# A decoder block on one core: ten of 22 tiles of the down projection by seven-product blocks, and the low parts of six early up weights by an accumulating transfer

## The chip, the cores and the metric

The kernel runs on one core of a Trainium2 chip. The metric is the device time of the whole program in microseconds (us); the median of three runs is 874.54 us (873.18 to 876.31). The engines are PE (matmul; PEld is its weight load), DVE (elementwise, two inputs), ACT (elementwise, one input), POOL and SP; SP issues nearly all loads. SBUF is the on-chip memory, PSUM holds eight banks of matmul results.

## The reference, cut to what matters

A decoder block over 512 tokens of width 1024. Two parallel branches (a recurrence and an attention), merged, are followed by a feed-forward part with 2816 channels, and only that part is touched:

```python
h2 = rmsnorm(x, norm2_g[l]) * (1.0 + scale2) + shift2
u = causal_dwconv(h2 @ w_up[l], ffn_conv_w[l], ffn_conv_b[l])
u_gate, u_val = u[..., :D_FF], u[..., D_FF:]
x = x + gate2 * ((jax.nn.silu(u_gate) * u_val) @ w_down[l])
...
return rmsnorm(x, final_g)
```

All inputs and the output are float32.

## The kernel before

**Number format.** Each matmul operand is held as two tiles: a rounded high part and the rest, the low part. `split` makes them: ACT copies the source into the high part (L207), DVE subtracts the high part from the source (L208). A product then takes three matmuls: high x high, high x low, low x high (L239 to L241 in the projections, L837 to L839 and L1228 to L1230 in the down projection).

**Weights.** `Stream` loads raw weights of 128 x 1024 (512 KB) into one of three `raw` buffers and splits them into tiles of 512 columns, alternately under the tags `whl` and `whg`, with two buffers each. A tile is written when PE has finished with the tile that lay in its buffer before.

**The up projection.** The 2816 gate channels and 2816 value channels are computed in 22 steps j, each with one tile of 128 channels of either kind; the result of step j (`ff[j]`, 128 channels x 512 tokens, high and low) is the left side of the down projection. In seven steps (`STRASSEN`, j = 5, 7, ... 17) the two tiles are already computed together by seven products of quarter blocks with matmuls of 256 columns (L1099). The first four tiles are multiplied for 256 tokens at a time. DVE adds the convolution taps (L1151) and gates (L1155, L1156). From j = 18 on DVE also forms the gate row `g2` (L556).

**The down projection.** 512 tokens x 2816 channels times 2816 x 1024 weights. The output columns are done in two halves of 512. In the first half each of the 22 tiles of 128 channels is multiplied with four blocks of 128 tokens into four banks (12 matmuls of 512 columns a tile); then `resid2` multiplies by `g2` and adds to the residual `x1` (L1202, L1203), and the first half's part of the final norm follows (L1218 to L1220). In the second half the same is done into five pieces (`parts`: three token blocks, and the fourth in two halves of 256 columns). The last `LASTK` = 8 tiles are held whole (`wl`), so that each piece can be finished by itself: its evacuation and norm (L1250 to L1259) and its output transfer lie beside the next piece's matmuls.

**Order.** Up to the feed-forward part the order of every queue is a table of numbers (`QUEUES`), which the change leaves alone. In the feed-forward part the order comes from the framework's scheduler, which goes by priorities (`tc.high_priority(offset=...)`) and its own costs. So a change of the code there can move any instruction of the stage. Every engine runs its queue in order.

## Time and profile before

| | |
|---|---|
| median of three runs | 874.54 us |
| the profiled execution | 876.59 us |
| its span, first to last instruction | 874.8 us |
| mean granted PE clock | 0.993 |
| PE's matmul instructions | 4282 |
| up projection, first matmul of it | 500.45 us after the span's start |
| down projection, first matmul to last | 744.30 to 866.77 us |
| last output transfer issued behind | 869.51 us + 0.75 (last scaling on DVE) |

Each row of a timeline gives start, duration, engine, line of the code, operation, output <- inputs by the names of the program's tiles, and in brackets how long the engine had stood idle and what ended that. Lines are those of the kernel before. A row of a stretch gives its length, then the busy time of PE, PEld, DVE, ACT and POOL (with the number of instructions), the granted clock, the DMA engines' share and GB/s. Matmuls overlap each other in the pipeline, so their pace is read from start to start.

### The profile page before, as it was taken

The numbers are of one execution on the slowest core, as the hardware profiler recorded it, in microseconds if no ns is written. First come the engines' busy times: TensorE is split into PE (matmuls) and PEld (weight loads), VectorE is DVE, ScalarE is ACT, GpSimd is POOL, SyncE is SP. The second block draws the span as 40 slices with busy tenths as digits, with TensorE's granted clock in tenths as the row PEclk, the third lists the DMA queues.
The fourth block names the chain that finished last, engine by engine and source line by source line (L and its number), as shares of the span: only waits on it lengthen the run. The fifth ranks groups of instructions, "written<-read, shape, count | busy, mean of one in ns | idle before, by whom it ended". The sixth has DMA issues, their size and how long they took to land.

```text
span 874.8 us, 11864 instructions
## 1 busy us (share of the span) xinstructions
PE 852.0 (97%) x4282; PEld 695.0 (79%) x4282; DVE 682.4 (78%) x1298; ACT 513.5 (59%) x953; POOL 18.7 (2%) x43
## 2 busy tenths in 40 slices
PE   7999999999999999999999999999999999999996
PEld 3777888888876777777877897888888887888885
DVE  6988888998965999997465779999999899424434
ACT  7485878677755798885244565566666654322323
POOL 0001000000020000000000000000000000000000
PEclk8999999999999999999999999999999999999998
DMA  9913233344472333454324032122332374322212
GB/s 344 354 67 106 72 111 111 108 146 118 153 183 97 119 122 130 139 176 157 97 75 164 5 118 97 62 98 103 104 102 105 104 241 145 120 93 89 93 65 96
DMA packets 33805, 109.09 MB, mean 125 GB/s; under 512 B 4290, under 2 KB 8002, under 8 KB 33748
## 3 DMA queue, kind: packets, MB, share of 16 engines
q1 hardware_dynamic: 32116, 103.60, 34.9%
q0 software_dynamic: 1632, 4.75, 2.3%
q8 instruction: 33, 0.54, 0.2%
q14 instruction: 24, 0.20, 0.1%
HBM read 103.59 MB, written 2.13 MB: 121 GB/s over the span
## 4 chain that ended last, share of the span: by engine, by line
PE 52%; DVE 25%; ACT 9%; DMA 7%; issue 5%; POOL 0%; SPq 0%; ACTq 0%; DVEq 0%; POOLq 0%
DVE whg L208 4%; DVE whl L208 3%; DVE Y L1151 3%; PE tr L241 3%; PE tr L240 3%; PE tr L239 3%; PE acc L241 2%; PE acc L239 2%; PE acc L240 2%; DMA raw<-in_w_up 2%; PE acc L837 2%; PE acc L839 2%; PE acc L838 2%; PE tr L741 2%; PE tr L1228 2%
## 5 line engine op out<-in xcount | busy, mean ns | idle before, releaser
L208 DVE TENSOR_TENSOR whl<-raw,whl 128x512 fp32r<-128x512 f32 (+2 forms) x138 | 85.6, 624 | 49.7 <-ACT whl L207 49.3
L207 ACT ACTIVATE whl<-raw 128x512 fp32r<-128x512 f32 (+2 forms) x138 | 78.7, 577 | 77.2 <-PE tr L241 22.6
L208 DVE TENSOR_TENSOR whg<-raw,whg 128x512 fp32r<-128x512 f32 x126 | 85.7, 687 | 37.3 <-ACT whg L207 37.0
L207 ACT ACTIVATE whg<-raw 128x512 fp32r<-128x512 f32 x126 | 77.8, 625 | 57.1 <-PE fil L839 22.0
L718 ACT ACTIVATE P<-P,mx,qsc 128x512 f32<-128x512 f32 (+3 forms) x64 | 41.2, 645 | 17.4 <-DVE mx L714 17.4
L239 PE MATMUL acc<-A,whg 128*128 128x512 f32 x120 | 47.9, 399 | 0.0
L240 PE MATMUL acc<-A,whg 128*128 128x512 f32 x120 | 47.4, 395 | 0.0
L241 PE MATMUL acc<-A,whg 128*128 128x512 f32 x120 | 47.4, 395 | 0.0
L1151 DVE SCALAR_TENSOR_TENSOR Y<-acc,vec,Y 128x511 f32<-128x511 f32 (+1 forms) x58 | 42.9, 744 | 3.6 <-ACT Y L1149 3.5
L239 PE MATMUL acc<-A,whl 128*128 128x512 f32 x104 | 41.1, 396 | 0.1
L240 PE MATMUL acc<-A,whl 128*128 128x512 f32 x104 | 41.1, 395 | 0.0
L241 PE MATMUL acc<-A,whl 128*128 128x512 f32 x104 | 41.1, 395 | 0.0
L239 PE MATMUL gm<-A,whg 128*128 128x512 f32 x88 | 35.5, 404 | 0.0
L241 PE MATMUL gm<-A,whg 128*128 128x512 f32 x88 | 35.1, 399 | 0.2 <-DVE whg L208 0.2
L240 PE MATMUL gm<-A,whg 128*128 128x512 f32 x88 | 35.3, 401 | 0.0
L239 PE MATMUL tr<-A,whl 128*128 128x512 f32 x80 | 32.6, 408 | 1.4 <-ACT whl L207 1.4
L241 PE MATMUL tr<-A,whl 128*128 128x512 f32 x80 | 32.2, 402 | 1.6 <-DVE whl L208 1.4
L711 DVE CUSTOM_DVE_ANT_0 P<-acc,mask 128x384 f32<-128x384 f32 (+3 forms) x64 | 28.6, 485 | 4.5 <-PE acc L708 4.1
L240 PE MATMUL tr<-A,whl 128*128 128x512 f32 x80 | 31.6, 394 | 0.0
L208 DVE TENSOR_TENSOR pt<-tr,pt 128x512 fp32r<-128x512 f32 (+1 forms) x48 | 27.4, 596 | 2.2 <-ACT pt L207 1.6
L741 PE MATMUL tr<-pt,v 128*128 128x512 f32 (+3 forms) x128 | 28.2, 328 | 0.1
L207 ACT ACTIVATE ff<-Y 128x512 fp32r<-128x512 f32 x22 | 13.9, 631 | 23.8 <-DVE Y L1156 23.1
(555 smaller groups left out, 2482.3 us busy)
## 6 DMA issues: line engine op xcount, KB each, us to landing
raw<-in_w_up SPq DMA_DIRECT2D x44, 512.0 KB, 3.6
raw<-in_w_dn SPq DMA_DIRECT2D x22, 512.0 KB, 3.5
wa<-in_w_adat SPq DMA_DIRECT2D x16, 512.0 KB, 9.4
raw<-in_w_adat SPq DMA_DIRECT2D x16, 512.0 KB, 3.3
raw<-in_w_xr SPq DMA_DIRECT2D x10, 512.0 KB, 3.9
raw<-in_w_pr SPq DMA_DIRECT2D x10, 512.0 KB, 3.6
raw<-in_w_gm SPq DMA_DIRECT2D x8, 512.0 KB, 4.1
raw<-in_w_gr SPq DMA_DIRECT2D x8, 512.0 KB, 3.5
```

Source lines behind the costliest of these rows:

```text
L207: S.activation(h, src, AF.Copy)
L208: return V.tensor_tensor(dst[:, 1, lo_c:lo_c + n], src, h.bitcast(F32), SUB).ins
L239: PE.matmul(out, wh, x[:, 0, xs], start=start, stop=False)
L240: PE.matmul(out, wh, x[:, 1, xs], start=False, stop=False)
L241: return PE.matmul(out, wl, x[:, 0, xs], start=False, stop=stop).ins
L711: V.tensor_tensor_reduce(out=pt[:, POFF[qd]:POFF[qd] + n], in0=sc[qd], in1=mask[:, T - n:], scale=1.0, scalar=-3e38, op0=ADD, op1=ALU.max, ...
L718: S.activation(pq, pq, AF.Exp, scale=qsc[:, qb:qb + 1], bias=mx[:, qb:qb + 1], accum_out=sm[:, qb:qb + 1])
L741: PE.matmul(yb[:, kb * P:], vv, pth[:, part, off:off + n], start=(i == 0 and part == 0), stop=(i == 3 and part == 1))
L837: PE.matmul(out, lt[:, 0, s], w[:, 0, :], start=start, stop=False)
L838: PE.matmul(out, lt[:, 0, s], w[:, 1, :], start=False, stop=False)
L839: return PE.matmul(out, lt[:, 1, s], w[:, 0, :], start=False, stop=stop).ins
L1151: V.scalar_tensor_tensor(u[:, d:], src[:, :T - d], vc("fw", (2 - d) * 2 * NF + cj), u[:, d:], MUL, ADD)
```

## The change

It has three parts.

1. *Down projection.* Of the 22 tiles, the last ten (`DPAIRS` = 5 pairs, tiles 12 to 21) are taken out of both column halves' ordinary loops (`KO` = 12 tiles stay there). For each pair the left side is a block of 2 token halves x 2 tiles, the right side 2 tiles x 2 column quarters of 256, and the block product is done with seven products of 2 x 3 matmuls of 256 columns instead of eight. `f_forms` makes the sums of the left side once, on DVE and ACT, during the ordinary tiles of the first half; they replace half of the pair's first `ff` tile and fill `fs`, in the place of `h2` (tag `A`). `w_forms` makes the differences of the right side for each pair and column half, partly in place in the raw tile, and splits them. The seven products accumulate over the five pairs in seven banks; the combination (L1282 to L1290), gate and residual (L1294, L1296) follow once a round. The first half's round comes behind its ordinary tiles, the second half's round ahead of its ordinary tiles. The fourth sum's sign: the tile kept for product 4 is the negative of the usual form, so its product is added.
2. *Last tiles.* `LASTK` is 6 instead of 8; `wl` stands in the place of `fs`.
3. *Early up weights.* For six tiles (`ADDS`, the `whg` tiles 9, 11, ... 19 of the up weights, used in steps 2 to 4) the low part is not made by DVE: ACT copies the high part, copies it again with the sign changed into the low part's place, and POOL issues a transfer that adds the raw weights from DRAM to it.

```diff
-LASTK = 8
+LASTK = 6
+DPAIRS = 5
+ADDS = tuple(range(9, 20, 2))
+LATE = 100
...
-                split(w, 0, self.cut, self.raws[r][:, o:o + self.cut])
+                if u in self.adds:
+                    S.activation(w[:, 0, :self.cut], self.raws[r][:, o:o + self.cut], AF.Copy)
+                    S.activation(w[:, 1, :self.cut], w[:, 0, :self.cut].bitcast(F32), AF.Copy, scale=-1.0)
+                    G.dma_start(w[:, 1, :self.cut], self.dram[r][:, o:o + self.cut], accum_op=ADD)
+                else:
+                    split(w, 0, self.cut, self.raws[r][:, o:o + self.cut])
...
+        KO = NF - 2 * DPAIRS
+        fs = st(sb, "A", 1, [P, DPAIRS, 3, 2, HT], F32R)
+        def f_forms(i):
+            f0, f1 = ff[KO + 2 * i], ff[KO + 2 * i + 1]
+            w = st(sb, "Y", 2, [P, 4, T])
+            for e, f in enumerate((f0, f1)):
+                V.tensor_tensor(w[:, e, :], f[:, 0, :].bitcast(F32), f[:, 1, :].bitcast(F32), ADD)
+            f11, f21, f12, f22 = (w[:, e, n * HT:n * HT + HT] for e in range(2) for n in range(2))
+            s1, s2, s3, s4 = (w[:, 2 + e, n * HT:n * HT + HT] for e in range(2) for n in range(2))
+            V.tensor_tensor(s1, f21, f22, ADD)
+            V.tensor_tensor(s2, s1, f11, SUB)
+            V.tensor_tensor(s3, f11, f21, SUB)
+            V.tensor_tensor(s4, f12, s2, SUB)
+            q = fs[:, i]
+            S.activation(q[:, 0:2, 0, :], halves(w[:, 2, :]), AF.Copy)
+            V.tensor_tensor(q[:, 0:2, 1, :], halves(w[:, 2, :]), q[:, 0:2, 0, :].bitcast(F32), SUB)
+            S.activation(q[:, 2, 0, :], s3, AF.Copy)
+            V.tensor_tensor(q[:, 2, 1, :], s3, q[:, 2, 0, :].bitcast(F32), SUB)
+            split(f0, HT, HT, s4)
...
+        def w_forms(c, i):
+            with tc.high_priority(offset=AHEAD):
+                r = raw()
+                dma(r, a["w_dn"][(c * NF + KO) // 2 + i])
+                q = [hl(sb, t, 2) for t in ("whl", "whg", "whl", "whg")]
+                split(q[0], 0, HT, r[:, :HT])
+                split(q[1], 0, T, r[:, T:])
+                low = halves(r[:, :T])
+                V.tensor_tensor(low, halves(r).rearrange("p (e f) n -> p e f n", f=2)[:, :, 1, :], low, SUB)
+                V.tensor_tensor(r[:, T + HT:], r[:, T + HT:], r[:, :HT], SUB)
+                V.tensor_tensor(r[:, T:T + HT], r[:, T:T + HT], r[:, T + HT:], SUB)
+                split(q[2], 0, T, r[:, :T])
+                split(q[3], 0, T, r[:, T:])
...
+        def strassen_down(c, tags):
+            b = {n: bank(tag, (P, 2, HT)) for n, tag in tags}
+            for i in range(DPAIRS):
+                f, w = forms[i], w_forms(c, i)
+                for n in ((1, 2, 3, 5, 7, 4, 6), (1, 2, 5, 3, 6, 7, 4))[i == DPAIRS - 1]:
+                    for e in range(2):
+                        s = slice(e * P, e * P + P)
+                        for m, (fe, we) in enumerate(((0, 0), (0, 1), (1, 0))):
+                            PE.matmul(b[n][:, e, :], f[n][:, fe, s], w[n][:, we, :], start=i == e == m == 0,
+                                      stop=i == DPAIRS - 1 and m == 2, skip_group_check=True)
+            y = st(sb, "Y", 2, [P, 4, 2, HT])
+            u, c11, p5, e = (y[:, n] for n in range(4))
+            u3 = st(sb, "Y", 2, [P, 4, 2, HT])
+            tmp, u3 = u3[:, 1], u3[:, 0]
+            S.activation(u, b[1], AF.Copy)
+            V.tensor_tensor(c11, b[2], u, ADD)
+            S.activation(p5, b[5], AF.Copy)
+            V.tensor_tensor(e, b[3], p5, ADD)
+            V.tensor_tensor(u, b[6], u, ADD)
+            V.tensor_tensor(u3, b[7], u, ADD)
+            V.tensor_tensor(e, e, u, ADD)
+            V.tensor_tensor(u, u3, b[4], ADD)
+            V.tensor_tensor(p5, p5, u3, ADD)
+            with tc.high_priority(offset=-LATE):
+                for n, x in enumerate((c11, e, u, p5)):
+                    o = c * T + n % 2 * HT
+                    V.tensor_tensor(tmp, x, g2[:, o:o + HT].unsqueeze(1).broadcast_to([P, 2, HT]), MUL)
+                    xs = x1p[n // 2][:, :, o:o + HT]
+                    V.tensor_tensor(xs, xs, tmp, ADD)
...
-        for k in range(NF):
+        for k in range(KO):
...
+            if k % 2 and k // 2 < DPAIRS:
+                f_forms(k // 2)
+        for t in range(4):
+            resid2(ob[t], t, 0)
+        strassen_down(0, ((1, "tr"), (2, "tr"), (5, "tr"), (3, "acc"), (6, "acc"), (4, "acc"), (7, "gm")))
...
+        strassen_down(1, ((1, "fil"), (2, "tr"), (3, "tr"), (5, "tr"), (7, "acc"), (4, "acc"), (6, "gm")))
...
-        for k in range(NF - LASTK):
+        for k in range(KO - LASTK):
```

How the order moves. First DVE around the end of the first column half. Before (`Y` is a scratch tile, `T` the residual, `acc` in second place the gate row `g2`):

```order
L208 TENSOR_TENSOR whl_7372<-raw_7370,whl_7372 128x512
L208 TENSOR_TENSOR whg_7390<-raw_7370,whg_7390 128x512
L208 TENSOR_TENSOR whl_7410<-raw_7408,whl_7410 128x512
L1202 TENSOR_TENSOR Y_7341<-acc_6979,acc_6690 128x512
L1202 TENSOR_TENSOR Y_7347<-acc_6980,acc_6690 128x512
L1203 TENSOR_TENSOR T_4208<-T_4208,Y_7341 128x512
L1203 TENSOR_TENSOR T_4208<-T_4208,Y_7347 128x512
L208 TENSOR_TENSOR whg_7428<-raw_7408,whg_7428 128x512
L1219 TENSOR_SCALAR s_7335<-s_7335 128x1
```

Now DVE at the change from the first round to the second (L1258 to L1260 are the differences of the right side, L1283 to L1290 the combination of the seven products, L1294 the gate):

```order
L211 TENSOR_TENSOR whl_7607<-raw_7605,whl_7607 128x256
L1283 TENSOR_TENSOR Y_7561<-tr_7260,Y_7561 128x512
L1258 TENSOR_TENSOR raw_7605<-raw_7605 128x512
L1294 TENSOR_TENSOR Y_7562<-Y_7561,acc_6696 128x512
L1285 TENSOR_TENSOR Y_7561<-acc_7262,Y_7561 128x512
L211 TENSOR_TENSOR whg_7608<-raw_7605,whg_7608 128x512
L1286 TENSOR_TENSOR Y_7561<-acc_7263,Y_7561 128x512
L1259 TENSOR_TENSOR raw_7605<-raw_7605 128x256
L211 TENSOR_TENSOR whl_7609<-raw_7605,whl_7609 128x512
L1260 TENSOR_TENSOR raw_7605<-raw_7605 128x256
L211 TENSOR_TENSOR whl_7666<-raw_7664,whl_7666 128x256
L1287 TENSOR_TENSOR Y_7562<-gm_7265,Y_7561 128x512
```

Where one split and then the residual stood, the combination now stands between the second round's splits, and a pair has three differences more.

Second, ACT at step 2 of the up projection, before:

```order
L207 ACTIVATE whl_4962<-raw_4960 128x512
L207 ACTIVATE ff_4889<-Y_4879 128x512
L207 ACTIVATE whg_4965<-raw_4960 128x512
L1149 ACTIVATE Y_4903<-fil_4654,vec_84 128x512
L207 ACTIVATE whl_5015<-raw_5013 128x512
L207 ACTIVATE ff_4897<-ff_4894 128x512
L207 ACTIVATE whg_5018<-raw_5013 128x512
L207 ACTIVATE ff_4898<-ff_4894 128x512
L1154 ACTIVATE Y_4903<-Y_4903 128x512
```

and now (L236 and L237 are the two copies):

```order
L210 ACTIVATE whl_4963<-raw_4961 128x512
L210 ACTIVATE ff_4889<-Y_4879 128x512
L236 ACTIVATE whg_4966<-raw_4961 128x512
L1157 ACTIVATE Y_4903<-fil_4654,vec_84 128x512
L237 ACTIVATE whg_4966<-whg_4966 128x512
L210 ACTIVATE whl_5017<-raw_5015 128x512
L1162 ACTIVATE Y_4903<-Y_4903 128x512
L210 ACTIVATE ff_4897<-ff_4894 128x512
L236 ACTIVATE whg_5020<-raw_5015 128x512
```

The second copy stands one or two instructions behind the first, and the transfer on POOL waits for it; the DVE split of the same tile is gone from DVE's queue.

Third, the end of DVE's queue. Before, from the third piece's norm to the last piece's addition (L304 to L311 are the norm, L1250 the gate on the piece's bank, L1258 the scaling of the output):

```order
L307 SCALAR_TENSOR_TENSOR rs_7770<-rs_7770,rs_7772 128x1
L311 SCALAR_TENSOR_TENSOR rs_7772<-rs_7770,rs_7772 128x1
L1250 TENSOR_TENSOR Y_7781<-gm_7368,acc_6690 128x256
L1258 SCALAR_TENSOR_TENSOR Y_7741<-T_4209,rs_7772,R_6976 128x512
L1251 TENSOR_TENSOR T_4209<-T_4209,Y_7781 128x256
L1255 SCALAR_TENSOR_TENSOR s_7338<-rs_7808,s_7338 128x1
L1250 TENSOR_TENSOR Y_7781<-acc_7369,acc_6690 128x256
L1251 TENSOR_TENSOR T_4209<-T_4209,Y_7781 128x256
L304 TENSOR_SCALAR rs_7839<-rs_7837,s_7338 128x1
```

and now:

```order
L312 TENSOR_SCALAR rs_8148<-rs_8146,s_7582 128x1
L313 RECIPROCAL rs_8150<-rs_8149 128x1
L315 SCALAR_TENSOR_TENSOR rs_8148<-rs_8148,rs_8150 128x1
L1348 TENSOR_TENSOR Y_8159<-acc_7923,acc_6696 128x256
L319 SCALAR_TENSOR_TENSOR rs_8150<-rs_8148,rs_8150 128x1
L1353 SCALAR_TENSOR_TENSOR s_7583<-rs_8180,s_7583 128x1
L1349 TENSOR_TENSOR T_4209<-T_4209,Y_8159 128x256
L1356 SCALAR_TENSOR_TENSOR Y_8125<-T_4209,rs_8150,R_6982 128x512
L312 TENSOR_SCALAR rs_8205<-rs_8203,s_7583 128x1
```

The last piece's gate (L1348 on `acc`) now stands ahead of the third piece's last norm step (L319), and that, the half's norm (L1353) and the third piece's scaling stand between or behind the last piece's two operations.

More of the change, by code (lines that the diff above doesn't have):

```diff
@@ L216, in block_kernel, with __init__ @@
     class Stream:
-        def __init__(self, dram, cols=1024, cut=512, alloc=w_both):
-            self.dram, self.cols, self.cut, self.alloc = dram, cols, cut, alloc
+        def __init__(self, dram, cols=1024, cut=512, alloc=w_both, adds=()):
+            self.dram, self.cols, self.cut, self.alloc, self.adds = dram, cols, cut, alloc, adds
             self.raws, self.hls = {}, {}
@@ L948, in block_kernel @@
             dma(xr[t], a["x"][t * P:(t + 1) * P, :])
-        x1 = [st(sb, "T", 2, [P, 2, D]) for _ in range(2)]
-        x1 = [x1[t // 2][:, t % 2, :] for t in range(4)]
+        x1p = [st(sb, "T", 2, [P, 2, D]) for _ in range(2)]
+        x1 = [x1p[t // 2][:, t % 2, :] for t in range(4)]
         ob = [bank(t) for t in ("acc", "acc", "acc", "gm")]
@@ L1030, in block_kernel @@
     with phase("p_ffn") as p3:
-        wu = Stream(a["w_up"], alloc=lambda u: hl(p3, "ff", NF) if u < 2 * EARLY - 2 else w_both(u))
+        wu = Stream(a["w_up"], alloc=lambda u: hl(p3, "ff", NF) if u < 2 * EARLY - 2 else w_both(u), adds=ADDS)
         ff = []
@@ L1205, in block_kernel, with halves @@
         wd = Stream(a["w_dn"])
+        KO = NF - 2 * DPAIRS
+        fs = st(sb, "A", 1, [P, DPAIRS, 3, 2, HT], F32R)
+        forms = []
+        def halves(x):
+            return x.rearrange("p (e n) -> p e n", n=HT)
+        def f_forms(i):
[15 more added lines that the diff above has]
+            split(f0, HT, HT, s4)
+            lo, hi = slice(0, HT), slice(HT, T)
+            forms.append({1: f0[:, :, lo], 2: f1[:, :, lo], 3: f0[:, :, hi], 4: f1[:, :, hi],
+                          5: q[:, 0], 6: q[:, 1], 7: q[:, 2]})
@@ new lines, in w_forms @@
+        def w_forms(c, i):
[11 more added lines that the diff above has]
+                split(q[3], 0, T, r[:, T:])
+            lo, hi = slice(0, HT), slice(HT, T)
+            return {1: q[0][:, :, lo], 2: q[1][:, :, lo], 3: q[1][:, :, hi], 5: q[2][:, :, lo], 7: q[2][:, :, hi],
+                    4: q[3][:, :, lo], 6: q[3][:, :, hi]}
@@ L1210, in block_kernel @@
             for t in range(4):
-                mm_tok(ob[t], ff[k], tok(t), w, k == 0, k == NF - 1)
+                mm_tok(ob[t], ff[k], tok(t), w, k == 0, k == KO - 1)
+            if k % 2 and k // 2 < DPAIRS:
[3 more added lines that the diff above has]
+        strassen_down(0, ((1, "tr"), (2, "tr"), (5, "tr"), (3, "acc"), (6, "acc"), (4, "acc"), (7, "gm")))
         s0 = [small(1, f"s0{t}") for t in range(4)]
@@ L1215, in block_kernel @@
         for t in range(4):
-            resid2(ob[t], t, 0)
             w = xf[t]
-            S.activation(w, x1[t][:, :T], AF.Square, accum_out=s0[t])
-            V.tensor_scalar(s0[t], s0[t], 1.0 / D, EPS, MUL, ADD)
-            V.scalar_tensor_tensor(w, x1[t][:, :T], -0.5, fg[:, :T], MUL, MUL)
+            with tc.high_priority(offset=-LATE):
+                S.activation(w, x1[t][:, :T], AF.Square, accum_out=s0[t])
+                V.tensor_scalar(s0[t], s0[t], 1.0 / D, EPS, MUL, ADD)
+                V.scalar_tensor_tensor(w, x1[t][:, :T], -0.5, fg[:, :T], MUL, MUL)
+        strassen_down(1, ((1, "fil"), (2, "tr"), (3, "tr"), (5, "tr"), (7, "acc"), (4, "acc"), (6, "gm")))
         parts = [(t, 0, T, bank("tr")) for t in range(3)]
-        parts += [(3, i * T // 2, T // 2, bank(b, (P, T // 2))) for i, b in enumerate(("gm", "acc"))]
+        parts += [(3, i * T // 2, T // 2, bank(b, (P, T // 2))) for i, b in enumerate(("fil", "acc"))]
         def mm_part(part, k, w, start, stop):
@@ L1236, in block_kernel @@
                 mm_part(part, k, w, k == 0, False)
-        wl = st(sb, "A", 1, [P, NK, 2, T], F32R)
+        wl = st(sb, "A", 1, [P, LASTK, 2, T], F32R)
         for i in range(LASTK // 2):
             r = raw()
-            dma(r, a["w_dn"][(2 * NF - LASTK) // 2 + i])
+            dma(r, a["w_dn"][(NF + KO - LASTK) // 2 + i])
             for e in range(2):
@@ L1247, in block_kernel @@
             for i in range(LASTK):
-                mm_part(part, NF - LASTK + i, wl[:, i], False, i == LASTK - 1)
+                mm_part(part, KO - LASTK + i, wl[:, i], False, i == LASTK - 1)
             c, cx = slice(o, o + n), slice(T + o, T + o + n)
```

## The prediction

> **What bounds the kernel now.** I read the page first (span, engines, slices), then the idle time of the matmul engine, then the feed-forward stage slice by slice.
>
> ```profile
> span 874.8 us, 11864 instructions
> PE 852.0 (97%) x4282; PEld 695.0 (79%) x4282; DVE 682.4 (78%) x1298; ACT 513.5 (59%) x953; POOL 18.7 (2%) x43
> PE   7999999999999999999999999999999999999996
> DVE  6988888998965999997465779999999899424434
> ```
>
> PE is busy from the second slice to the last. DVE stands at 9 in slices 25 to 34 (the up projection, about 525 to 745 us) and at 2 to 4 in the down projection behind them. So PE's own work sets the time, and DVE is close behind it in the up projection only. The stretches say the same, with their busy time:
>
> ```profile
> 540.00:560.00 20.00, 19.85 (x94) 16.09 (x94) 19.54 (x30) 11.79 (x20) 0.00 (x0) 1.00 0.17 54
> 560.00:580.00 20.00, 19.47 (x115) 16.85 (x114) 19.55 (x33) 11.58 (x21) 0.00 (x0) 1.00 0.32 106
> 760.00:780.00 20.00, 20.00 (x89) 16.28 (x88) 4.85 (x7) 4.43 (x7) 0.00 (x0) 1.00 0.25 80
> ```
>
> (Columns: length, then PE, PEld, DVE, ACT, POOL busy, clock, DMA.) In the down stretch DVE works 4.85 of 20 us and waits for PE to free weight buffers; around 560 it works 19.55. The clock is 1.00 in all three, so the clock needs no term. PE's waits, in order of time:
>
> ```profile
> 563.92 0.50 PE L1099 MATMUL tr<-A,whg 128*128 128x256 f32 x2
> 564.95 1.45 PE L1099 MATMUL tr<-A,whg 128*128 128x256 f32 x10 [0.53 <-DVE whg L208]
> 583.10 1.63 PE L1099 MATMUL tr<-ff,whl 128*128 128x256 f32 x12
> 585.36 1.81 PE L1099 MATMUL acc<-ff,whg 128*128 128x256 f32 x12 [0.63 <-ACT Y L1129]
> 602.47 1.56 PE L1099 MATMUL acc<-A,whg 128*128 128x256 f32 x12
> 603.87 1.59 PE L1099 MATMUL tr<-A,whl 128*128 128x256 f32 x12
> 605.29 1.60 PE L1099 MATMUL tr<-ff,whg 128*128 128x256 f32 x12
> 744.30 0.39 PE L837 MATMUL acc<-whl,ff 128*128 128x512 f32 x1
> 861.29 0.28 PE L1228 MATMUL gm<-A,ff 128*128 128x256 f32 x1
> 864.09 0.28 PE L1228 MATMUL acc<-A,ff 128*128 128x256 f32 x1
> 866.77 0.28 PE L1230 MATMUL acc<-A,ff 128*128 128x256 f32 x1
> ```
>
> Busy means of matmuls overlap, so I price them from start to start. The down projection runs from 744.30 to 866.77 and 0.12 more: 122.59 us for 22 tiles x 4 token blocks x 3 x 2 column halves = 528 matmuls of 512 columns, 0.2322 us each. Of 256 columns, 24 stand between 861.29 and 864.09: 0.1167 each; runs of 12 in the up projection's seven-product tiles take 1.40 and 1.42 (602.47, 603.87, 605.29): 0.1183 at most.
>
> **The matmuls replaced.** In each column half ten of the 22 tiles, 10 x 4 x 3 = 120 matmuls of 512, become five pairs of 7 products x 6 = 210 matmuls of 256. Both halves: 240 x 0.2322 = 55.7 us go. At 0.1183, 420 cost 49.7: **-6.0 us**. Ends: 0.1167 gives -6.7. For the other end I take the dearest stretch of such tiles, with its switch of banks and a wait for a copy inside:
>
> ```profile
> 606.73 1.80 PE L1099 MATMUL acc<-ff,whl 128*128 128x256 f32 x12
> 608.36 1.58 PE L1099 MATMUL tr<-A,whg 128*128 128x256 f32 x12
> ```
>
> 605.29 to 608.36 is 24 matmuls in 3.07 us, 0.128 each: 420 cost 53.7, so -2.0. I take a value near the first end, since a product here has no copy inside it; the switch after 6 rather than 12 matmuls is in neither row, and is why I keep 0.1183.
>
> A rule speaks against the change. The Trainium skill, "TensorE: Matmul & The Clock Gate", section "Back-to-back issue gap", gives a sustained spacing of about 81 ns at 128 columns and 131 ns at 512, so that halving the width saves far less than half; between them an estimate for 256 is 98 ns. By it the sum would be 420 x 0.098 - 240 x 0.131, about +9.7 us, instead of -6.0. The trace disagrees: 0.1167 against 0.2322.
>
> **DVE as the feeder of the new rounds.** One pair needs, per column half, splits of 256, 512, 512, 512 columns, a difference of 512 and two of 256: seven DVE instructions. DVE also overlaps; its rows from start to start:
>
> ```profile
> 570.42 0.42 DVE L1131 TENSOR_TENSOR Y<-tr,Y 128x256 f32<-128x256 f32 x1
> 570.76 0.41 DVE L1136 TENSOR_TENSOR Y<-tr,Y 128x256 f32<-128x256 f32 x1
> 711.85 0.69 DVE L208 TENSOR_TENSOR whg<-raw,whg 128x512 fp32r<-128x512 f32 x1
> 712.45 0.69 DVE L208 TENSOR_TENSOR ff<-Y,ff 128x512 fp32r<-128x512 f32 x1
> 753.00 0.63 ACT L207 ACTIVATE whl<-raw 128x512 fp32r<-128x512 f32 x1 [2.18 <-PE fil L839]
> 753.66 0.69 DVE L208 TENSOR_TENSOR whl<-raw,whl 128x512 fp32r<-128x512 f32 x1 [2.12 <-ACT whl L207]
> ```
>
> So 0.60 us for 512 columns and 0.34 for 256: a pair costs DVE 4 x 0.60 + 3 x 0.34 = 3.42 us while PE spends 42 x 0.1183 = 4.97 on it. The two weight tags have two buffers each, just one pair, so a buffer that PE frees must pass ACT (0.63) and DVE (0.69), 1.35 us by the last two rows, before the next pair's product, which comes 3.5 us after the release. That leaves some 2 us of slack.
>
> - *The forms of the left side* (`f_forms`: per pair three DVE instructions of 512 and six of 256, 3 x 0.60 + 6 x 0.34 = 3.84 us, 19.2 in all) stand beside the first twelve ordinary tiles, 12 x 12 x 0.2322 = 33.4 us, in which DVE has 12 x 0.60 = 7.2 us of splits and, up to about 750, the last gates. That fits, and the splits run four tiles (11 us of PE) ahead. Cost 0; were DVE some 10 us later there, PE would begin to wait.
> - *First round*: 5 x 3.42 and eight residual operations of 0.60 are 21.9 us in 24.9. I take +0.2 for its start.
> - *Second round*: the order puts 52 DVE instructions between its first split and the split for its last buffer: 20 of 512 and 15 of 256 for the weights, and 17 more, which are the first round's evacuation (13 of 512), two of 512 and two tiny ones for the norm. Sum 35 x 0.60 + 15 x 0.34 + 0.2 = 26.3 us. Time for it: from 4.2 us before the round (PE frees the first buffer) less 0.5 for ACT, to the fifth product of the fifth pair, 4 x 4.97 + 4 x 0.71 = 22.7: together 26.4. So no slack is left at the end, while some instructions wait for ACT. I take **+1.0**; ends 0, and 4.3 if every instruction costs its full 0.69 or 0.42 (35 x 0.69 + 15 x 0.42 + 0.2 = 30.7 against 26.4).
> - The banks of the rounds are freed by reads that stand ahead of the products that need them, and SP issues as many loads of `w_dn` as before, 22. The last six tiles' weights (`wl`) now wait for the second round's end, but six tiles x 12 x 0.2322 = 16.7 us of matmuls cover their splits (6 x 0.60) and the rest of the evacuation (15 x 0.60). Cost 0; the cover fails only if DVE comes more than 3 us late.
>
> **Early up weights.** Six tiles lose a DVE split (6 x 0.60 = 3.6 us off the DVE backlog that reaches from 520 to past 585) and gain an ACT copy and a transfer. The two waits of PE in the rows above go, I say: start to start they are 564.95 - 563.92 - 2 x 0.118 = 0.79 and 585.36 - 583.10 - 12 x 0.118 = 0.84 us (shown as 0.53 and 0.63 of idle time). The first is for a DVE split; in the second ACT comes late, and ACT, 11.58 of 20 us busy there, has itself mostly waited for DVE. I take **-1.4**, for a rest of 0.1 each may stay; ends -1.6 and 0. The added copies lie in ACT's idle time (8 of 20 us). POOL waits for the second copy, and behind it on POOL stand only the other five transfers; for the landing PE waits. Its cover:
>
> ```profile
> 535.42 0.63 ACT L207 ACTIVATE whg<-raw 128x512 fp32r<-128x512 f32 x1 [2.23 <-PE acc L241]
> 543.93 0.40 PE L239 MATMUL acc<-A,whg 128*128 128x512 f32 x1
> q<-rp POOLq DMA_DIRECT2D x16, 128.0 KB, 2.7
> yr<-rd POOLq DMA_DIRECT2D x8, 256.0 KB, 6.4
> raw<-in_w_up SPq DMA_DIRECT2D x44, 512.0 KB, 3.6
> ```
>
> A buffer freed at 535.42 is used at 543.93, its low part 0.47 later: 8.98 us. Two copies and one operation between them take 3 x 0.63 = 1.9, so 7 us are left for issue and landing. No row has an accumulating transfer; POOL's others land in 2.7 to 6.4, the 256 KB ones, which queue eight deep, last. I take 4 (nearest to the single ones): hidden, cost 0; the upper end 6.4 is hidden too.
>
> **The tail.**
>
> ```profile
> 866.55 0.16 DVE L1255 SCALAR_TENSOR_TENSOR s<-rs,s 128x1 f32<-128x1 f32 x1 [0.58 <-ACT Y L1253]
> 867.08 0.42 DVE L1250 TENSOR_TENSOR Y<-acc,acc 128x256 f32<-128x256 f32 x1 [0.38 <-PE acc L1230]
> 867.54 0.42 DVE L1251 TENSOR_TENSOR T<-T,Y 128x256 f32<-128x256 f32 x1
> 868.00 0.42 ACT L1253 ACTIVATE Y<-T 128x256 f32<-128x256 f32 x1 [1.49 <-DVE T L1251]
> 869.51 0.75 DVE L1258 SCALAR_TENSOR_TENSOR Y<-T,rs,R 128x512 f32<-128x512 f32 x1
> ```
>
> With six instead of eight last tiles the third block's norm is not done when PE ends: the order sets two tiny instructions between the last product and its addition (2 x 0.2), and the third block's copy ahead of the last square on ACT. **+0.4**, ends 0 and 1.0.
>
> **Sum.** -6.0 + 0.2 + 1.0 - 1.4 + 0.4 = -5.8 us. The profiled execution took 876.59 (span 874.8 and 1.8 around it), so it would take 870.8; the median of the runs is 874.54, 2.05 below it, and so **868.7**.
>
> **Rivals.**
> 1. *DVE bounds the second round* at its full durations: +4.3 and +0.3 in the first instead of +1.2: 872.1. For it: no slack in the sum. Against: around 560 DVE works 19.55 of 20 us at these pitches.
> 2. *Slower: the accumulating transfers come late.* Tile u needs the buffer of tile u-4, so with a landing d beyond 7 us three of the five late ones stall by d each (a stall gives the next one time). At 10 us that is 9 us, and the 1.4 are not won: 879.1. It decides from 7 + 4.4/3 = 8.5 us on. For it: no row shows such a transfer. Against: the longest POOL row is 6.4.
> 3. *The relief is not won*: the two waits stay since ACT, given 6 more copies, or a raw tile's transfer ends last there: 870.1.
> 4. *A half-wide matmul does not cost half* in this mix, and each waits for its own weight load, 188 ns in the rows of PEld: 420 x 0.188 = 79 us against 55.7, +23: over 890. The page on TensorE above points that way. The runs of 12 in 1.40 us refute it in the same mix of loads.
>
> ```profile
> L239 PEld LDWEIGHTS acc<-A,whl 128*128 128x128 f32 x104 | 19.6, 188 | 4.5 <-ACT ff L207 0.5
> ```
>
> **How the numbers follow.** Forecast 54%, rival 1 15%, rival 2 9%, rival 3 17%, rival 4 2%, the rest unnamed. 0.3%, 2.6 us, is about what a measurement of this kernel tells from no change. Forecast and rival 3 are faster by more than that, rival 1 falls just inside it, 2 and 4 are slower; with a tail of the forecast moved inside the bound: faster 0.74, same 0.15, slower 0.11. The ends of the terms span -6.7 - 1.6 = -8.3 (866.2) to rival 1's 872.1 and a little above, when -6.0 is short; the range 865.8 to 873.6 leaves out rivals 2 and 4 and half of the unnamed.
>
> **What would show it.** Products of 6 matmuls at 0.70 to 0.71 us in the new rounds; DVE near 9 tenths there, and PE's waits in the second round's last pair, on a split into `whg`; the two waits in the up projection gone; POOL's six transfers landing in 3 to 5 us; 3.1 us instead of 869.51 - 866.77 = 2.74 from PE's last start to the last scaling. Wrong it would be by waits of PE on `whg` between 530 and 560, by waits in every pair of the second round, or by spacings over 0.13.

## The result, and the profile after

The changed kernel took 868.82 us (median of four runs, 867.90 to 870.13) beside 874.06 us for the kernel before (four runs, 873.18 to 876.31): ratio 0.9937, 95% interval 0.9913 to 0.9961. The forecast was 868.7 us. The time came out as forecast, but two terms of the sum were wrong by about a microsecond each, in opposite directions. Two disturbed executions are left out below: the profiled one of the kernel pool_gate (2181 us, while its other five took 867.2 to 869.1), so that no stages are given for it, and one of swap67 (911 us). The lines of the code after the change stand higher: L207 and L208 are now L210 and L211, L1099 is L1107, L1250 is L1348 and L1258 is L1356.

The page of the changed kernel, span, engines and the slices of DVE:

```profile
span 868.3 us, 12376 instructions
PE 845.7 (97%) x4432; PEld 698.3 (80%) x4432; DVE 737.1 (85%) x1417; ACT 534.8 (62%) x998; POOL 23.9 (3%) x49
DVE  7989888988856899998375679999989999998985
```

PE, busy in 97% of the span, is still the bound. DVE has 55 us more to do (682.4 before), and its slices 35 to 40, which read 424434, now read 998985. The stretches of the two rounds say how close that is (length, then PE, PEld, DVE, ACT and POOL busy, clock, DMA):

```profile
775.25:800.04 24.79, 24.79 (x211) 24.78 (x210) 22.52 (x43) 12.28 (x22) 0.00 (x0) 1.00 0.34 107
800.04:825.60 25.56, 25.11 (x212) 24.86 (x211) 25.27 (x51) 13.72 (x27) 0.00 (x0) 1.00 0.30 94
```

DVE works 22.52 of 24.79 us in the first round and 25.27 of 25.56 in the second. Both contain 210 matmuls of the products; the second is 0.8 us longer. The one idle time of DVE in the second round is 0.26 us, and what ended it is a square for the norm on ACT:

```profile
818.43 0.15 DVE L1316 TENSOR_SCALAR s<-s 128x1 f32<-128x1 f32 x1 [0.26 <-ACT R L1315]
```

PE's timeline shows the marks of the stages and the place of that wait:

```profile
500.43 0.37 PE L247 MATMUL acc<-A,ff 128*128 128x256 f32 x1
741.98 0.39 PE L845 MATMUL acc<-whl,ff 128*128 128x512 f32 x1
775.03 0.39 PE L847 MATMUL fil<-whg,ff 128*128 128x512 f32 x1
775.25 0.87 PE L1276 MATMUL tr<-whl,ff 128*128 128x256 f32 x6
775.96 0.89 PE L1276 MATMUL tr<-whg,ff 128*128 128x256 f32 x6
822.79 0.28 PE L1276 MATMUL gm<-whg,A 128*128 128x256 f32 x1
823.52 0.86 PE L1276 MATMUL gm<-whg,A 128*128 128x256 f32 x5 [0.45 <-DVE whg L211]
859.24 0.28 PE L1328 MATMUL acc<-A,ff 128*128 128x256 f32 x1
```

The up projection (500.43 to 741.98) takes 241.55 us, 243.85 before. The down projection, from its first matmul's start to its last one's, takes 117.26 us, 122.47 before. All waits of PE that the profile names from the up projection on:

```profile
PE gm L1276 <- DVE whg L211: 0.5, 1, 0.5
PE acc L1107 <- DVE whg L211: 0.4, 1, 0.4
PE acc L1107 <- DVE whl L211: 0.3, 1, 0.3
```

None is on an accumulating transfer. These land in 4.5 us in the median, the first of them in 6.35, the others in 4.1 to 4.7 (the row of the transfers: count, size, median from issue to landing):

```profile
whg<-in_w_up POOLq DMA_DIRECT2D x6, 256.0 KB, 4.5
```

The tail is the part that looks otherwise than forecast. On DVE, the scaling of the first piece, the gate of the third and the last scaling:

```profile
852.49 0.75 DVE L1356 SCALAR_TENSOR_TENSOR Y<-T,rs,R 128x512 f32<-128x512 f32 x1
857.98 0.69 DVE L1348 TENSOR_TENSOR Y<-tr,acc 128x512 f32<-128x512 f32 x1 [2.89 <-DMA out_y<-Y]
863.50 0.75 DVE L1356 SCALAR_TENSOR_TENSOR Y<-T,rs,R 128x512 f32<-128x512 f32 x1
```

The last scaling starts 4.26 us after PE's last matmul (863.50 - 859.24), 2.74 before. DVE stood idle for 2.89 us ahead of the third piece's gate, and what ended that is the first piece's output transfer: the pieces share two `Y` buffers, so the third may write only when the first has been read. That transfer was issued at 853.31 and landed 4.6 us later, where the first one of the kernel before took 2.6; the second piece's was issued 1.85 us behind it, instead of 4.3 before.

### The profile page after: what moved, and what is told of

The parts are those of the page before. It is cut to its first block, busy times and chain, and to the rows that moved or that the text cites. A ratio compares the mean times of both kernels' runs of the same rounds, so it can differ in the third digit from the quotient of the medians.

```text
span 868.3 us, 12376 instructions
## 1 busy us (share of the span) xinstructions
PE 845.7 (97%) x4432; PEld 698.3 (80%) x4432; DVE 737.1 (85%) x1417; ACT 534.8 (62%) x998; POOL 23.9 (3%) x49
## 4 chain that ended last, share of the span: by engine, by line
PE 55%; DVE 20%; ACT 10%; DMA 9%; issue 4%; POOL 0%; SPq 0%; ACTq 0%; DVEq 0%; POOLq 0%
PE acc L249 5%; PE acc L248 5%; PE acc L247 5%; PE tr L249 3%; PE tr L247 3%; PE tr L248 3%; DVE whg L211 3%; PE acc L1107 2%; DVE whl L211 2%; DMA wa<-in_w_adat 2%; PE tr L1107 2%; PE tr L749 2%; PE gm L249 2%; DVE Y L1159 1%; PE gm L247 1%
## 5 line engine op out<-in xcount | busy, mean ns | idle before, releaser
L210 ACT ACTIVATE whl<-raw 128x512 fp32r<-128x512 f32 (+2 forms) x149 | 83.6, 566 | 69.6 <-PE tr L249 22.4
L211 DVE TENSOR_TENSOR whl<-raw,whl 128x512 fp32r<-128x512 f32 (+2 forms) x149 | 90.6, 612 | 23.3 <-ACT whl L210 22.8
L210 ACT ACTIVATE whg<-raw 128x512 fp32r<-128x512 f32 x131 | 80.9, 625 | 44.5 <-PE tr L249 9.1
L211 DVE TENSOR_TENSOR whg<-raw,whg 128x512 fp32r<-128x512 f32 x131 | 89.2, 688 | 17.8 <-ACT whg L210 17.4
L210 ACT ACTIVATE ff<-Y 128x512 fp32r<-128x512 f32 (+1 forms) x27 | 15.9, 590 | 22.0 <-DVE Y L1164 20.8
L211 DVE TENSOR_TENSOR pt<-tr,pt 128x512 fp32r<-128x512 f32 (+1 forms) x48 | 27.5, 596 | 2.1 <-ACT pt L210 1.6
```

The lines of the kernel that those rows point to most:

```text
L210: S.activation(h, src, AF.Copy)
L211: return V.tensor_tensor(dst[:, 1, lo_c:lo_c + n], src, h.bitcast(F32), SUB).ins
```

## The experiments

Each ratio is to the kernel before, run beside it; its median was 874.06 us beside the changed kernel, 874.15 beside the next four rows of the table, 873.14 beside the four behind them and 873.84 beside the last four, so that medians of different groups do not compare to better than 1 us. In code that no kernel here touches, the start of the up projection varies from 496.4 to 500.5 us between profiled executions. So I read small effects from the stage lengths, each of one profiled execution (up projection; down projection from first to last matmul start; tail from there to the last scaling), and use the ratio for the whole. The up projection takes 241.31 to 242.19 us in the eight kernels that have the same instructions in the same order there, so differences below 0.9 us in it say nothing.

| kernel | median us | ratio (95%) | up | down | tail |
|---|---|---|---|---|---|
| before | 874.06 | 1 | 243.85 | 122.47 | 2.74 |
| changed | 868.82 | 0.9937 (0.9913 to 0.9961) | 241.55 | 117.26 | 4.26 |
| adds_alone | 871.77 | 0.9977 (0.9967 to 0.9987) | 241.60 | 122.44 | 2.75 |
| rounds_alone | 869.35 | 0.9952 (0.9936 to 0.9967) | 244.25 | 116.94 | 3.93 |
| third_buffer | 867.44 | 0.9922 (0.9908 to 0.9937) | 242.19 | 117.27 | 2.75 |
| pool_gate | 868.07 | 0.9932 (0.9918 to 0.9946) | | | |
| after_again | 867.79 | 0.9933 (0.9918 to 0.9949) | 241.81 | 117.27 | 4.29 |
| last8 | 865.93 | 0.9916 (0.9898 to 0.9935) | 241.75 | 117.27 | 2.75 |
| pairs3 | 873.45 | 0.9998 (0.9984 to 1.0012) | 241.55 | 125.33 | 2.97 |
| pool_combo | 866.17 | 0.9917 (0.9899 to 0.9935) | 241.54 | 117.76 | 3.18 |
| swap67 | 868.72 | 0.9935 (0.9917 to 0.9952) | 241.31 | 117.35 | 3.91 |
| best | 866.76 | 0.9916 (0.9899 to 0.9933) | 241.58 | 117.33 | 2.75 |
| adds12 | 872.69 | 0.9984 (0.9972 to 0.9996) | 245.12 | 116.96 | 4.25 |
| adds_early | 866.19 | 0.9912 (0.9896 to 0.9929) | 241.19 | 116.97 | 3.95 |

**The two parts by themselves.** The kernel before with the six transfers alone:

> The kernel before with the six accumulating transfers alone; the down projection is the old one, with eight last tiles. Theory (the changed kernel's up projection is shorter because VectorE does six subtractions fewer early in it): from the start of the up projection to that of the down projection 241.6 us (243.85 before, 241.55 in the changed kernel), the rest as before, so 874.1 - 2.3 = 871.8 us, ratio 0.9974. Rival (the up projection is shorter because the scheduler also placed the work of the two rounds otherwise, and the transfers gain nothing by themselves): 243.9 us for the up projection and 874.1 us in all. Rival (the transfers cost PE something that the rounds' gain hid): above 874.1 us, with PE waiting on an accumulating transfer.

And the changed kernel with `ADDS = ()`:

> The changed kernel without the accumulating transfers: the ten tiles in Strassen's products remain, all up weights are split by ScalarE and VectorE. Theory (the two parts of the change add up): up projection 243.9 us, down projection's last matmul start 117.3 us after its first as in the changed kernel, so 868.8 + 2.3 = 871.1 us, ratio 0.9966 to the kernel before. Rival (the up projection's gain belongs to the rounds): 868.8 us. If the backlog of VectorE at the end of the up projection reached into the down projection, it would be above 871.5 us, with a PE wait before the first round.

PE's marks and its longest waits, first of the transfers alone, then of the rounds alone:

```profile
497.35 0.36 PE L244 MATMUL acc<-A,ff 128*128 128x256 f32 x1
738.94 0.39 PE L842 MATMUL acc<-whl,ff 128*128 128x512 f32 x1
PE acc L1104 <- DVE whg L208: 0.6, 2, 0.4
```

```profile
497.54 0.37 PE L247 MATMUL acc<-A,ff 128*128 128x256 f32 x1
741.79 0.39 PE L845 MATMUL acc<-whl,ff 128*128 128x512 f32 x1
PE acc L1107 <- ACT Y L1137: 0.6, 1, 0.6
PE tr L1107 <- DVE whg L211: 0.5, 1, 0.5
PE gm L1276 <- DVE whg L211: 0.3, 1, 0.3
```

The transfers alone make the up projection 241.60 us, 2.25 less, and leave the rest as it was. Without them it is 244.25 and the two waits that the prediction showed (on a split, and on ACT's copy at L1129, now L1137) are both back. So this gain belongs to the transfers, and the rival that it came from another order of the work falls. For the rounds alone I expected 871.1 us and measured 869.35. The stages agree with the theory (244.25 against 243.9, 116.94 against 117.3, a tail shorter by 0.3). The early part of the program varies by more than the 1.8 us, and in the profiled execution the up projection starts 2.9 us earlier than in the changed kernel's; that this is the cause is not shown. The expected ratio, 0.9966, lies within the interval. The product of the two ratios, 0.9929, lies within the intervals of the whole change's, 0.9937 and here 0.9933:

> The changed kernel once more, beside the runs of this call. Theory (the parts add up: transfers alone gave 871.8 us, so 2.4 us, and the rounds alone 869.35 us, so 4.8 us): 874.15 - 2.4 - 4.8 = 867.0 us, or 868.8 us as in its first four runs if the rounds alone only came out low; in the trace 241.6 us of up projection and 117.3 us of down projection either way. Rival (the transfers are worth less in the presence of the rounds): 868.8 us and an up projection longer than 241.6 us.

The stages repeat within 0.3 us (241.81, 117.27, 4.29), and the parts add up.

rounds_alone also shows how the wait in the second round comes about. There, and in adds12 and adds_early below, DVE goes through the round in the same order, but the square on ACT comes 0.28 us earlier and DVE does not stand idle for it: PE's wait is 0.29 us instead of 0.45, and the round takes 25.3 us instead of 25.6. So PE's wait follows DVE's queue. Why ACT is earlier there, the traces do not show.

**The tail.** Two ways to take the wait of the third piece away: another tag's buffer for it,

```diff
-                w = st(sb, "Y", 2, [P, 2, T])
+                w = st(sb, "R", 4, [P, 2, T]) if t == 2 else st(sb, "Y", 2, [P, 2, T])
```

> The changed kernel with the third of the last pieces in a buffer of another tag, so that its gate no longer waits until the first piece's output transfer has read its buffer. Theory (this wait, 2.89 us on VectorE, is why the tail grew from 2.74 to 4.26 us from the last matmul's start to the last scaling): the third gate starts with its matmuls' end, the tail is 2.7 to 3.1 us again, time 868.8 - 1.3 = 867.5 us. Rival (six tiles a piece instead of eight give VectorE too little time for three chains, whatever the buffer): the tail stays at 3.9 us or more and the time at 868.8 us.

and `LASTK = 8`, so that eight instead of six tiles lie between the pieces' ends:

> The changed kernel with eight resident tiles at the end instead of six, so pieces 5.6 us apart instead of 4.2. Theory (the third piece's gate waits for the first piece's output transfer only because the pieces come close together): the gate of the third piece waits for PE, the tail is 2.75 us and the time 868.8 - 1.5 = 867.3 us. Rival (four streamed tiles, 11.1 us, are too short a cover for eight tiles to be split while VectorE still works on the second round's combination): PE waits on a split into A at the start of the last pieces, by 1 us or more, and the time is 868.8 us or above.

DVE's gate of the third piece and its last scaling, and PE's last matmul, first with the other buffer, then with eight tiles:

```profile
854.93 0.69 DVE L1348 TENSOR_TENSOR R<-tr,acc 128x512 f32<-128x512 f32 x1 [0.27 <-PE tr L1328]
858.82 0.28 PE L1328 MATMUL acc<-A,ff 128*128 128x256 f32 x1
861.57 0.75 DVE L1356 SCALAR_TENSOR_TENSOR Y<-T,rs,R 128x512 f32<-128x512 f32 x1
```

```profile
851.56 0.69 DVE L1348 TENSOR_TENSOR Y<-tr,acc 128x512 f32<-128x512 f32 x1 [1.66 <-PE tr L1328]
856.84 0.28 PE L1328 MATMUL acc<-A,ff 128*128 128x256 f32 x1
859.59 0.75 DVE L1356 SCALAR_TENSOR_TENSOR Y<-T,rs,R 128x512 f32<-128x512 f32 x1
```

Either way the gate waits for PE, as it should, and the tail is 2.75 us. With the other buffer there are still six tiles a piece, so it was the buffer and not DVE's time for three chains. Eight tiles cost nothing ahead of them: the down projection is 117.27 us, and no wait on a split into `A` shows. The rival of each falls. The buffer is worth 1.5 us by the trace; in the times the intervals overlap.

The wait also depends on how long the first piece's transfer takes. It lands in 4.6 us in changed, after_again and adds12, with tails of 4.25 to 4.29, and in 3.3 in rounds_alone, swap67 and adds_early, with tails of 3.91 to 3.95. With eight tiles the second piece's transfer is issued 3.8 us behind it instead of 1.85, and it lands in 2.6; but it does so in pairs3 below too, with 1.85, so what lengthens it the runs do not show. In third_buffer it took 3.3; there the fourth piece follows the first in its `Y` buffer, so that kernel is not safe from a transfer of 4.6, as pool_combo below shows.

**The wait in the second round.** First, one quarter of the first round's gate and residual on POOL (`G` for the first of the four, with a temporary of its own), alone and together with the other buffer:

> The changed kernel with one quarter of the first round's gate and residual (two of eight instructions of 128x512) on GpSimd instead of VectorE. Theory (the 0.5 us wait of PE in the second round's last pair is VectorE's queue, which has the first round's combination and gate in it): two instructions fewer are 1.2 us of queue, the wait of 0.5 us goes, the second round takes 24.9 us instead of 25.6, time 868.2 us. Rival (GpSimd's instructions of this size hold VectorE up while they run): VectorE's 128x512 subtractions of the second round show more than 0.69 us, the round takes 25.6 us or more, and the time is 868.8 us or above.

> The changed kernel with the third piece in another tag's buffer (867.4 us alone) and a quarter of the first round's gate and residual on GpSimd (868.1 us alone). Theory: the tail is 2.75 us, the wait of 0.5 us in the second round's last pair is gone and that round takes 24.9 us; 867.4 - 0.6 = 866.8 us. Rival (GpSimd's instructions hold VectorE's up): its subtractions of 128x512 in the second round take more than 0.69 us in the mean and the wait stays; 867.4 us or above.

In the combined kernel the second round takes 26.08 us, not 24.9, and PE's wait in the last pair is still there (`gm` on a split, 0.4 us). DVE's instructions there, and POOL's two beside them:

```profile
793.58 0.68 DVE L1258 TENSOR_TENSOR raw<-raw 128x512 f32<-128x512 f32 x1
794.18 0.69 DVE L1285 TENSOR_TENSOR Y<-acc,Y 128x512 f32<-128x512 f32 x1
794.84 1.14 DVE L211 TENSOR_TENSOR whg<-raw,whg 128x512 fp32r<-128x512 f32 x1
795.90 0.68 DVE L1286 TENSOR_TENSOR Y<-acc,Y 128x512 f32<-128x512 f32 x1
796.50 0.92 DVE L1259 TENSOR_TENSOR raw<-raw 128x256 f32<-128x256 f32 x1
```

```profile
793.80 1.62 POOL L1294 TENSOR_TENSOR Y<-Y,acc 128x512 f32<-128x512 f32 x1 [248.29 <-DVE Y L1283]
795.51 1.63 POOL L1296 TENSOR_TENSOR T<-T,Y 128x512 f32<-128x512 f32 x1
```

The last two DVE instructions with both inputs in SBUF (L211, L1259) end 0.56 and 0.28 us after POOL's (795.42 and 797.14), and take 1.14 for 0.69 and 0.92 for 0.42; the two with an input in PSUM (L1285, L1286) keep 0.69 and 0.68. POOL's own two end 1.16 us behind DVE's instructions of that kind (793.58 + 0.68 = 794.26, and 795.98). That reads as two engines taking turns. The Trainium skill, "SBUF — State Buffer", section "SBUF: two separate sides", has DVE and GpSimd share one port pair as an exclusive lock, which a DVE instruction with two SBUF inputs needs against a GpSimd one that reads SBUF, and which goes to the one that starts first. By that page the one that starts later waits for the other's end, and the trace agrees, 0.92 against 0.42 us on DVE. So 1.0 of the 1.2 us saved was given back. The other half of my theory failed too: the scheduler set other work of DVE (a norm step, the next tile's split) into the place, and the split that PE waits for in the last pair came 0.5 us later in the round, not earlier. The times, 868.07 and 866.17 us, are nearer the theories' 868.2 and 866.8 than the rivals', but differences of 0.6 us lie within the intervals here; the trace shows the rival's mechanism. The tail of 3.18 instead of 2.75 has again a wait of 1.19 us for an output transfer in it, now ahead of the fourth piece's gate: with the third piece elsewhere it is the fourth that follows the first in its `Y` buffer.

Then, the sixth and seventh product exchanged in the last pair, so that the late split is needed 0.7 us later:

```diff
-                for n in ((1, 2, 3, 5, 7, 4, 6), (1, 2, 5, 3, 6, 7, 4))[i == DPAIRS - 1]:
+                for n in ((1, 2, 3, 5, 7, 4, 6), (1, 2, 5, 3, 7, 6, 4))[i == DPAIRS - 1]:
```

> The changed kernel with the sixth and seventh product exchanged in each round's last pair, so that the product which needs the last split weight comes 0.7 us later. Theory (the 0.6 us that PE loses in the second round's last pair is one subtraction late by that much, and the next weights are in time): that wait is gone, the second round takes 25.0 us instead of 25.6, the down projection 116.7 us instead of 117.3; the time is 0.6 us below the changed kernel's. Rival (VectorE is the bound of the whole second round, so that the lost time turns up at the next split): 25.6 us with the wait on a split a product or a tile later.

The second round now takes 24.91 us, as the theory had it. But the down projection takes 117.35, not 116.7, since right behind the round a new wait stands, on ACT's copy of a product out of the bank that the next piece needs:

```profile
823.43 0.50 PE L1326 MATMUL tr<-whl,ff 128*128 128x512 f32 x1 [0.54 <-ACT Y L1284]
```

From start to start that wait costs 0.70 us (823.43 - 822.61 - 0.12), as much as the round gained. ACT itself works only 13.72 of 25.56 us in the second round (in the changed kernel); what made it late is DVE again, whose last gate of the first round still read the `Y` buffer that ACT's copies write:

```profile
821.78 0.60 ACT L1282 ACTIVATE Y<-fil 128x512 f32<-128x512 f32 x1 [0.43 <-DVE Y L1294]
```

So the rival was nearer: the 0.8 us is not one late split but the end of a round in which DVE has no slack, and it shows at the next thing that PE needs from it, directly or through ACT. With eight tiles in addition:

> The changed kernel with eight resident tiles and the exchanged products. Theory (both losses are apart from each other): the tail 2.75 us and the second round 25.0 us, so 2.1 us below the changed kernel, ratio to the kernel before 0.9915. Rival (the last weights' splits, eight now, meet the round's combination on VectorE): the wait on a split appears at the last pieces, and the gain over the changed kernel is 1.5 us or less.

It has the tail of 2.75 us and the wait at L1326. Its ratio, 0.9916, is that of last8 alone, and so are its stages within 0.2 us, so the exchange is worth nothing.

**Fewer pairs.** `DPAIRS = 3`:

> The changed kernel with three pairs of tiles in each round instead of five. Theory (each pair saves 48 matmuls of 0.2322 us for 84 of 0.1183 us, 1.2 us, and the combination is paid once for any number of pairs): the down projection is 2.4 us longer, 119.7 us, plus what VectorE cannot do of the first round's combination in a round of 15 us instead of 25, some 0 to 3 us: 871.2 to 874.2 us, 872 us the likeliest. Rival (VectorE sets the rounds' length, so that fewer pairs cost nothing): 868.8 us.

The time falls into the expected range (873.45, as slow as the kernel before), but by another sum. The down projection is 8.1 us longer than with five pairs. The smaller saving is 2.5 of it. Behind the second round, 15.25 us long, PE waits for DVE, which is not through with the first round's gate and so holds the `Y` buffer for the second's copies. The waits, and then the stretches (PE's granted clock is the column behind the five engines):

```profile
PE fil L1326 <- ACT Y L1282: 2.1, 1, 2.1
PE acc L1327 <- DVE whl L211: 0.7, 1, 0.7
```

```profile
817.26 0.60 ACT L1282 ACTIVATE Y<-fil 128x512 f32<-128x512 f32 x1 [2.68 <-DVE Y L1294]
819.99 0.63 PE L1328 MATMUL tr<-whl,ff 128*128 128x512 f32 x1
820.42 0.63 PE L1326 MATMUL tr<-whl,ff 128*128 128x512 f32 x1
```

```profile
806.00:815.50 9.50, 8.76 (x70) 8.17 (x69) 9.46 (x19) 4.80 (x10) 0.00 (x0) 1.00 0.48 141
815.50:817.90 2.40, 0.29 (x2) 0.08 (x1) 2.33 (x5) 0.64 (x2) 0.00 (x0) 0.80 0.78 237
817.90:823.50 5.60, 5.59 (x16) 4.63 (x17) 3.80 (x9) 1.94 (x6) 0.00 (x0) 0.50 0.09 36
823.50:830.00 6.50, 6.50 (x31) 5.39 (x30) 5.14 (x9) 1.62 (x3) 0.00 (x0) 0.98 0.24 69
```

The waits cost 3.1 us, from start to start. Then PE's clock stands at 0.50 for 5.6 us: the spacing of matmuls is 0.43 us (819.99 to 820.42) instead of 0.2322, and that costs 2.8 us more (16 matmuls in 5.9 us that take 3.1 at full pace). The Trainium skill, "TensorE: Matmul & The Clock Gate", section "What's actually happening", tells of a clock that is halved after an idle window of about 3.4 us. Here the clock fell sooner: its mean of 0.80 over 815.50 to 817.90 puts the fall some 1.0 us before the end of the wait, when PE had stood idle for about 1.2 us, with 0.7 us of another wait shortly before. In this kernel the waits so cost nearly twice what they last. That is no rule: in adds12 below, PE stands idle for 1.7 and then for 2.0 us, 9 us apart, and the granted clock stays at 1.00 from 566 to 585 us. The runs do not show what decides. The three parts make 8.4 us, and the second round's own delay is 0.4 us shorter than with five pairs, which leaves 8.0 of the 8.1. The rival, that DVE sets the rounds' length and fewer pairs cost nothing, falls.

**More transfers.** For tiles up to the 31st, and for every tile from 8 to 19:

```diff
-ADDS = tuple(range(9, 20, 2))
+ADDS = tuple(range(9, 32, 2))    # in adds12
+ADDS = tuple(range(8, 20))       # in adds_early
```

> The changed kernel with twelve accumulating transfers, one for every second tile up to the 31st, instead of six up to the 19th. Theory (the transfers gain what VectorE's backlog makes PE wait, and the six have left 0.7 to 0.9 us of such waits in the up projection): up projection 241.0 us instead of 241.6, the time 0.6 us below the changed kernel's. Rival (every removed subtraction is worth as much as the first six, 0.4 us): up projection 239.3 us. Rival (among the later tiles' work the transfers land late): PE waits on them and the up projection is longer than 241.8 us.

Only two of the six added numbers are tiles of the stream (the others belong to the seven-product steps); eight transfers show. Those two are enough to make the up projection 3.6 us longer. POOL's issues of the two, the wait, and the landing:

```profile
564.05 0.86 POOL L238 DMA_DIRECT2D whg<-in_w_up  x1 [16.95 <-PE acc L1107]
573.49 0.87 POOL L238 DMA_DIRECT2D whg<-in_w_up  x1 [8.58 <-ACT whg L237]
PE acc L249 <- DMA whg<-in_w_up: 3.7, 2, 2.0
whg<-in_w_up POOLq DMA_DIRECT2D x8, 256.0 KB, 4.5
```

The landing is the same 4.5 us, but here a seven-product step lies between, whose weights go through the same two buffers. The first of these two buffers comes free for the ACT copy at 562.46, the transfer goes out at 564.05, and PE wants the low part at 566.87: 2.8 us of room instead of 7. This is the prediction's rival of late transfers, at tiles that the change leaves to DVE.

> The changed kernel with accumulating transfers for each of the tiles 8 to 19 instead of every second. The room that a transfer has is then shared by two, one each 2.75 us. Theory (a landing of 4.5 us has room for 7 us, and the next one on GpSimd's queue need not wait for it): no PE wait on a transfer, and no gain over the six, since the waits that are left lie after these tiles: up projection 241.5 us. Rival (a weight buffer is free only when the tile two before is done, so the chain of two copies and one transfer, 5.8 us with no tile between that is made otherwise, does not fit into the 5.5 us of two tiles): PE waits on the transfers at most of the twelve tiles, 0.3 to 1.5 us each, up projection 244 us or more.

Twelve transfers in the same tiles do fit; the landing of half of them grows only to 5.2 us:

```profile
whl<-in_w_up POOLq DMA_DIRECT2D x6, 256.0 KB, 4.6
whg<-in_w_up POOLq DMA_DIRECT2D x6, 256.0 KB, 5.2
```

PE has no named wait left between the start of the up projection and that of the down projection, and the former is 241.19 us. That is within 0.2 us of the shortest of the eight kernels with six transfers (241.31, in swap67), so a gain over six is not shown, as the theory had it. The rival's chain did not hold PE up. Its ratio, 0.9912, is the best seen, though its interval overlaps that of most kernels here; together with eight tiles at the end it was not tried.

## Why the prediction was right, and where it was not

| term | predicted us | measured us | from |
|---|---|---|---|
| matmuls replaced | -6.0 | -6.2 | 420 x 0.1180 - 240 x 0.2322 |
| start of the first round | +0.2 | 0.0 | 775.03 to 775.25 is one matmul |
| wait in the second round | +1.0 | +0.8 | 25.59 - 24.79 |
| early up weights | -1.4 | -2.3 | 241.55 - 243.85; -2.25 alone |
| tail | +0.4 | +1.5 | 4.26 - 2.74 |
| behind the last scaling | none | -0.5 | 4.77 - 5.25 |
| sum | -5.8 | -6.7 | spans: 868.3 - 874.8 = -6.5; medians: -5.2 |

- *Matmuls.* 210 matmuls in the 24.79 us of the first round are 0.1180 us each; the products start 0.71 us apart. That a half-wide matmul costs half was the step on which most hung, and it held; the rival by which it costs more falls.
- *DVE as the feeder.* The balance of 26.3 us of work in 26.4 us of time was right to the place: no wait in the first round, and one in the second round's last pair on the split into `whg`. The clause "while some instructions wait for ACT" held as well: 0.26 us of DVE's time went that way, and without it PE's wait is 0.29 us. What the step did not say is that the second round's copies on ACT hang on DVE too, through the `Y` buffer, so that moving the late split (swap67) moves the wait. The rival at DVE's full durations falls: at 0.60 us a piece DVE fits.
- *Early up weights.* The step that failed on the small side: "The two waits of PE in the rows above go, I say", with an end of -1.6. I priced only the two largest waits. The kernels with and without the transfers differ by 2.25 and 2.7 us, because a backlog costs PE also in small pieces. Counted start to start over the whole up projection, delays over 0.15 us add up to 2.7 us before and 1.15 after, and the remaining 0.8 us of the gain lies in shorter ones. Of the two waits the second did not go: 0.52 of its 0.84 us start to start (0.37 of idle time) is left, now on a split, so the two gave 1.1 us and not 1.4, and the other 1.2 us of the gain lies in delays that I had put at nothing. (0.5 us of the 2.25 is a wait at 736 us in the kernel before, which rounds_alone, without the transfers, does not have either.)
- *The transfer hidden.* I took 4 us, with 7 us of room; the transfers landed in 4.5 us in the median, and PE waited for none. The rival's mechanism is real, as adds12 shows, but not at these tiles.
- *Tail.* The step that failed on the dear side: "the order sets two tiny instructions between the last product and its addition", +0.4. I followed DVE's and ACT's order and never asked who still reads the buffer that the third piece writes. With pieces 4.2 us apart instead of 5.6, the first piece's output transfer does. The two tiny instructions themselves cost nothing: with the other buffer the tail is 2.75 us, as before, with the same six tiles.
- The -0.5 us behind the last scaling was in no term, and the runs do not explain it; this stretch is 4.77 in most profiles here and 5.25 to 5.74 in the kernel before, adds_alone and rounds_alone.

So the mechanism held in the two terms of the rounds, each within 0.2 us, and the total agreed because +1.1 in the tail and -0.9 in the up projection nearly cancel. That 868.82 lies within 0.1 us of the forecast is luck: the terms measured add up to 0.9 us more of gain than the terms forecast, while the medians moved by 5.2 us, with an interval of 3.4 to 7.6.

## What to carry to other kernels

Where a stage is cut into shorter pieces, ask of every rotating buffer who reads it last, the output transfer included: the wait shows on the engine that writes it, not where the piece was cut. A backlog on a feeding engine costs PE more than its few visible waits add up to; price its relief by all delays start to start. And when an engine is full to the last microsecond of a stage, moving one late item moves the wait; what shortened it here was 0.26 us less idle time of that engine.

## What the runs showed of the hardware that I had not expected

- PE's granted clock fell to 0.50 some 1.2 us into an idle time of 2.1 us, with 0.7 us of another shortly before, and stayed there for 5.6 us behind the wait (pairs3); the waits cost 3.1 us and the slow clock 2.8. Idle times of 1.7 and 2.0 us left it at 1.00 (adds12).
- A POOL instruction of 128x512 (1.62 us) held up DVE's instructions with two SBUF inputs until it ended (1.14 us for 0.69, 0.92 for 0.42), and not those with an input from PSUM; POOL's own ended 1.16 us behind such instructions of DVE (pool_combo).
- An accumulating transfer of 256 KB from POOL's queue lands in 4.5 us in the median, in 4.6 and 5.2 (the medians of the two tags) when twelve follow each other every few microseconds, with an issue of 0.87 us on POOL.
- The first of two output transfers of 512 KB issued 1.85 us apart landed in 4.6 us in four of the kernels, in 3.3 in four and in 2.6 in one (pairs3); the runs do not show why.
